# A hybrid decoder step: page loads shared differently between two queues, and four edits of order around them

## The chip, the core and the metric

The kernel runs on one core of a Trainium2 chip. A core has five engines, each with its own instruction queue that is worked in order: TensorE (PE, matmuls), VectorE (DVE), ScalarE (ACT), GpSimd (POOL) and SyncE (SP, which here only issues DMAs). ScalarE and POOL issue DMAs too, between their own instructions. The metric is the device time of one execution in microseconds (us).

## The reference, cut to what matters

One layer of a decoder runs for a prompt of 1024 rows and 8 x 4 sample rows, 1056 in all. Its first half, where the change lies:

```
h = rmsnorm(x, g_norm1) * (1 + scale1) + shift1
za, zq, zkv, zg, zm = jnp.split(h @ w_in, SPLIT_IDX, axis=-1)
u, v = jnp.split(jax.nn.gelu(za), 2, axis=-1)
vn = layernorm(v, ln_v_g, ln_v_b)
ya = chunk_spatial_gating(u, vn, w_spatial, b_spatial)
...
kv_rows = jnp.concatenate([past_rows, paged_new], axis=1)
...
kc = compress_blocks(rows[:, :, :, 0], cmp_pe[0], cmp_w1[0], cmp_b1[0], cmp_w2[0], cmp_b2[0])
vc = compress_blocks(rows[:, :, :, 1], cmp_pe[1], cmp_w1[1], cmp_b1[1], cmp_w2[1], cmp_b2[1])
p_cmp = masked_softmax(jnp.einsum('btkgd,bnkd->btkgn', qg, kc), avail[None, :, None, None, :])
...
gate_a, gate_b = jnp.split(jax.nn.sigmoid(zm), 2, axis=-1)
mixed = (gate_a * (ya @ w_branch_a) + gate_b * (yb @ w_branch_b)) @ w_out
```

For the samples `past_rows` are 8 sequences of 8192 cached rows, and `compress_blocks` makes one key and one value of each 64 rows. The best blocks by `p_cmp` are then attended in full, and a window of 512 rows beside them. After it come the residual, a second norm, the up-projection with a width-3 convolution, the down-projection and a last norm. All is in float32; a big product is made of three float32r products (upper x upper, upper x lower, lower x upper).

## The kernel before, in words

**Compression of the cache (`step`, lines 546 to 664).** The 8 x 8192 cached rows are compressed in 16 steps, numbered 0 to 15. A step takes 32 pages of 128 KB (`pcmp`), all into the one buffer `st`, so the pages of step n+1 are issued only when the 64 matmuls of step n (`compress`) have read it. `step(n)` runs these matmuls, the gelu on ScalarE (`compress_act`, L569), and the issue of the next pages (`compress_load`, `load_pages`, L538). The pages come in eight groups of four. The tuple `share` names the groups that ScalarE issues, (1, 4, 6), and SyncE issues the others. Before, step 5's pages were all left to SyncE. For each group the queue reads four page numbers into registers (L528) and issues four DMAs; a group waits until the group two before it on the same queue has landed, and each issue for an earlier DMA of its lane.

**What lies between the steps.** From about 183 us the u outputs of the gMLP follow (loop with L704 to L722): for each j of 4, 72 products of 384 or 288 columns, then 9 small matmuls of the spatial gating. Steps 3 and 4 stood behind j = 1 and j = 3. Then come 11 pairs (loop at L967) for queries, merge gates and keys. A `pair` makes two outputs of 128 x 1056 by a Strassen-like scheme: the weights' quarters a11, a12, a21, a22 (raw tiles, loaded on ScalarE's queue, L873) give the sums s1 to s4 on POOL (L892 to L897). The activations' quarters give T2, T3, T4 and B12, once (`sums_of`, `last_sums`, on DVE, POOL and ScalarE). Each weight tile is split by a cast on ScalarE (L332) and a subtraction on DVE (L333) into three rotating buffers. A "product" is 12 matmuls: of 304 columns on a quarter, or of 448 on the rest columns (`rest`, `plain`). The scheduler, not the code alone, sets the place of the instructions on each engine. `step(5)` to `step(14)` stand inside pairs 0 to 9, after the a11 and a12 products.

**The start of attention (L1018 to L1063, and from L1209).** The queries lie in memory (`q_d`). The first of the eight tiles of 128 queries is read on its own (`qf`), the four full query tiles `qt` follow, then the values `VV`. `key_tiles` splits the keys, `queries` a tile's queries. The four buffers of `page_buffer` take in turn a chunk of `w_ada` (late modulation), the window cache (`wk`, `wv`) and selected pages (`psel`). Here the code's order holds on TensorE: compressed scores of the first tile, scores of unit 0, unit 1, the first `w_ada` product, and on.

Of the kernel before, what the change touches and what calls it, by code (L numbers as in the profile page):

```python
# [6 lines left out]
F32 = mybir.dt.float32  # L7
# [46 lines left out]
def step_kernel(tc, A):  # L54
# [48 lines left out]
    S = new_pool("slots")  # L103
    NS = 24

    def slot(dt=F32):
        return S([128, R], dt, "S", NS)
# [438 lines left out]
    def compress_load(n):  # L546
        b, half = n // 2, n % 2
        home = "a"
        st = PG([128, 32, 256], F32, "st", 1)
        load_pages([(st[:, i], A["pcmp"], b * 64 + half * 32 + i) for i in range(32)], freed.get(home),  # L550
                   () if n == 5 else (1, 4, 6))
        paged[n] = st, home

    def compress(n):
# [146 lines left out]
    for j in range(4):  # L701
        u = slot()
        dense(A["w_t"][j], 8, hh, hl,
              lambda a, b, ps, u=u: act.activation(u[:, a:b], ps, AF.Gelu_apprx_tanh))  # L704
        for s in range(3):
            w = 512 if s < 2 else 32
            ps = pT()
            tmp = RV2([128, 512], F32, "sg", 2)
            if s < 2:
                for i in range(4):  # L710
                    mm(ps[:, 128 * i:128 * i + 128], vn[4 * s + i][:, 128 * j:128 * j + 128], wsp[:, j], True, True)
                dve.tensor_tensor(tmp.rearrange("p (i t) -> p i t", t=128),
                                  ps.rearrange("p (i t) -> p i t", t=128),
                                  bsp[:, j, None, :].to_broadcast([128, 4, 128]), op=OP.add)
            else:
                mm(ps[:, 0:32], vn[8][:, 128 * j:128 * j + 128], wsps[:, j].rearrange("p b t -> p (b t)"), True, True)
                dve.tensor_tensor(tmp[:, 0:32].rearrange("p (b t) -> p b t", t=4),
                                  ps[:, 0:32].rearrange("p (b t) -> p b t", t=4),
                                  bsp[:, j, None, 0:4].to_broadcast([128, 8, 4]), op=OP.add)
            uc = u[:, 512 * s:512 * s + w]  # L720
            pool.tensor_tensor(uc, uc, tmp[:, 0:w], op=OP.mult)  # L721
        pool.dma_start(ya_d[j], u)  # L722
        if j % 2:
            step(3 + j // 2)
    RV2.release()
    RV.release()
# [131 lines left out]
    def quarter_products(w, x, ps, first, last):  # L858

        for k in range(4):  # L860
            hi, lo = x[k]
            mm(ps, w[0][k], hi, first and k == 0, False, not (first and last))
            mm(ps, w[0][k], lo, False, False, not (first and last))
            mm(ps, w[1][k], hi, False, last and k == 3, not (first and last))

    rest = [tuple(t[:, 2 * HQ:R] for t in (hh[k], hl[k])) for k in range(8)]

    def pair(m, n, ev, closing=False):

        raws = []  # L870
        for j, c in ((m, 0), (m, 512), (n, 0), (n, 512)):
            raws.append(W([128, 512], F32, "raw", 4))
            act.dma_start(raws[-1], A["w_t"][j][:, c:c + 512])  # L873
        a11, a12, a21, a22 = raws
        g, t = out_tile(), out_tile()
        first, second, third = slice(0, HQ), slice(HQ, 2 * HQ), slice(2 * HQ, R)
        plain = [pA()[:, 0:R - 2 * HQ] for _ in range(2)]
        X, S, Z = pA()[:, 0:HQ], pT()[:, 0:HQ], pT()[:, 0:HQ]
        add = lambda o, x, y: dve.tensor_tensor(o, x, y, op=OP.add)  # L879
        s1, s2 = sum_tile(0), sum_tile(1)  # L880

        w = weight_parts(a11)
        quarter_products(w, rest[0:4], plain[0], True, False)
        quarter_products(w, B11, X, True, True)
        act.copy(g[:, first], X)
        w = weight_parts(a12)
        quarter_products(w, rest[4:8], plain[0], False, True)
        quarter_products(w, B21, X, False, True)
        ev(t[:, third], plain[0])
        ev(t[:, first], X)  # L890
        yield
        pool.tensor_tensor(s1, a21, a22, op=OP.add)  # L892
        pool.tensor_tensor(s2, s1, a11, op=OP.subtract)
        quarter_products(weight_parts(a21), rest[0:4], plain[1], True, False)
        s3, s4 = a21, a12
        pool.tensor_tensor(s3, a11, a21, op=OP.subtract)
        pool.tensor_tensor(s4, a12, s2, op=OP.subtract)  # L897
        if closing:
            w = weight_parts(a22)
            quarter_products(w, rest[4:8], plain[1], False, True)  # L900
            ev(g[:, third], plain[1])
            Y = pA()[:, 0:HQ]
            quarter_products(w, T4, Y, True, True)
            quarter_products(weight_parts(s1), B12, Z, True, True)
            ev(g[:, second], Z)
            quarter_products(weight_parts(s4), B22, Z, False, True)
            ev(t[:, second], Z)
            w = weight_parts(s2), weight_parts(s3)
            quarter_products(w[0], T2, S, True, True)
            for o in (t, g):  # L910
                add(o[:, second], g[:, first], o[:, second])
            add(t[:, second], S, t[:, second])
            quarter_products(w[1], T3, S, False, True)
            add(g[:, first], Y, g[:, first])
            add(g[:, second], S, g[:, second])
            add(g[:, first], S, g[:, first])
            yield t, g
            return
        quarter_products(weight_parts(s2), T2, S, True, True)
        add(t[:, second], S, g[:, first])  # L920
        quarter_products(weight_parts(s3), T3, S, False, True)
        add(g[:, second], S, g[:, first])
        quarter_products(weight_parts(s1), B12, Z, True, True)
        add(g[:, second], Z, g[:, second])
        w = weight_parts(a22)
        quarter_products(w, T4, S, False, True)
        add(g[:, first], S, g[:, first])
        ev(g[:, 0:2 * HQ], g[:, 0:2 * HQ])
        quarter_products(w, rest[4:8], plain[1], False, True)
        ev(g[:, third], plain[1])  # L930
        quarter_products(weight_parts(s4), B22, Z, False, True)
        add(t[:, second], Z, t[:, second])
        ev(t[:, second], t[:, second])
        yield t, g
# [32 lines left out]
    for i in range(11):  # L967
        j = 2 * i
        m, fn, ev, base = ((4 + j, query, scaled, 4) if i < 2 else (6 + j, merge_gate, gate, 10) if i < 10 else
                           (8, key, lambda o, x: act.copy(o, x), 8))  # L970
        work = pair(m, m + 1, ev) if i < 10 else pair(9, 8, ev, True)
        next(work)
        if i == 0:
            for k in range(4):
                sums_of(k)
            last_sums()
        if i < 10:
            step(n)
            n += 1
        out = next(work)  # L980
        for x, j in zip(out, (m - base, m + 1 - base)) if i < 10 else zip(out[::-1], range(2)):
            fn(j, x)
        if i in (5, 6, 7, 8):
            next(first_blocks, None)
# [17 lines left out]
    def queries(i, l, qf=None):  # L1002

        c0 = 128 * i
        qs = slot(F32R)
        dve.tensor_copy(qs[0:1, 0:1], l[0:1, 0:1].bitcast(F32))
        for j in range(4):
            q = qf[:, 128 * j:128 * j + 128] if qf is not None else qt[j][:, c0:c0 + 128]
            for h in range(2):
                own, other = slice(64 * h, 64 * h + 64), slice(64 - 64 * h, 128 - 64 * h)  # L1010
                c = (4 * h + j) * 128
                act.copy(qs[own, c:c + 128], q[own])
                dve.tensor_tensor(qs[other, c:c + 128], q[own], qs[own, c:c + 128].bitcast(F32), op=OP.subtract)
        return qs


    qf = W([128, 512], F32, "raw", 4)
    sync.dma_start(qf.rearrange("p (j c) -> p j c", j=4),  # L1018
                   q_d[:, :, 128 * TILES[0]:128 * TILES[0] + 128].rearrange("j p c -> p j c"))
    key_tiles(0)  # L1020
    q_first = queries(TILES[0], KL[0][0], qf)
    compress_act(*compress(15))
    PG.release()
    TR.release()
# [19 lines left out]
    def page_buffer():  # L1044

        n = len(uses)
        uses.append(None)
        assert n < 4 or uses[n - 4] is not None
        return n, R3S([128, 4, 4, 256], F32, f"st{n % 4}", 1), uses[n - 4] if n >= 4 else None

    YS = R3([128, 8, 32])

# [164 lines left out]
    def qtile(i):  # L1217
# [3 lines left out]
        c0 = 128 * i  # L1221
        ps = pM()
        for j in range(4):
            mm(ps[:, 32 * j:32 * j + 32], qt[j][:, c0:c0 + 128], kcb.rearrange("p h n -> p (h n)"), True, True)
        s = R3([128, 8, 16], F32, "cs", 2)
        dve.tensor_tensor(s, ps[:, 0:128].rearrange("p (a n) -> p a n", n=16),
                          cmpadd[:, i, None, :].to_broadcast([128, 8, 16]), op=OP.add)
# [848 lines left out]
```

## Time and profile before

| | us |
|---|---|
| median of three runs | 2006.5 |
| lowest, highest | 2002.08, 2008.75 |
| the profiled execution | 2004.65 |
| its span, first to last instruction | 2003.1 |
| TensorE busy | 1857.2 (93%) |
| DVE, ScalarE, POOL busy | 1240.0, 836.4, 612.4 |
| mean granted TensorE clock | 0.969 of full speed |

A row of the views reads: engine, line of the kernel, operation, output and input tiles, shape, count; in brackets the idle time of the engine before it and what ended it. "ACTq" and "SPq" are the sequencers of ScalarE and SyncE, where DMAs are issued. q1 is SyncE's DMA queue, q10 ScalarE's, q0 POOL's. A window's row gives the stretch, busy time (and count) by engine, the granted clock, the share of the DMA engines and GB/s.

### The profile page before, as it was taken

The page shows a single profiled execution, that of the slowest core. Times are in us where ns is not written, and L with a number is a line of the kernel's source. Part 1 is how long each engine was busy: PE and PEld are TensorE (multiplying, and loading weights), DVE is VectorE, ACT ScalarE, POOL GpSimd, SP SyncE. Part 2 cuts the span into 40 slices and gives each one's busy share as a digit, 9 for nine tenths or more (in the row PEclk, how much of TensorE's full clock was granted, in tenths as well). Part 3 has the DMA queues.
Part 4 walks back from the last instruction along what each step waited for, and adds up shares of the span by engine and source line. Part 5 has one row for each costly group of instructions (what it writes and reads, how often), then busy time and mean ns, then how long its engine had stood idle before and what let it go on. Part 6 is the DMA issues. An engine that isn't in the chain of part 4 may idle for free.

```text
span 2003.1 us, 43803 instructions
## 1 busy us (share of the span) xinstructions
PE 1857.2 (93%) x15905; PEld 1725.1 (86%) x15905; DVE 1240.0 (62%) x2547; ACT 836.4 (42%) x1706; POOL 612.4 (31%) x805
## 2 busy tenths in 40 slices
PE   5999969889989699999999999999999999999998
PEld 3999958878878577676779999999999999999997
DVE  7526163223323476767666667999988888757464
ACT  4313122212222365465564247644444444545343
POOL 2410242112113113223220331188766665301010
PEclk8999989989989799999999999999999999999999
DMA  8546455465564657887775535333322222677464
GB/s 322 186 135 190 139 164 191 144 197 168 164 191 154 225 192 239 285 257 224 228 254 182 200 126 162 113 100 115 108 98 76 86 76 90 212 242 215 138 193 112
DMA packets 241848, 345.36 MB, mean 172 GB/s; under 512 B 35264, under 2 KB 173408, under 8 KB 239456
## 3 DMA queue, kind: packets, MB, share of 16 engines
q1 hardware_dynamic: 186928, 243.17, 38.3%
q0 software_dynamic: 17808, 58.16, 8.1%
q10 hardware_dynamic: 36896, 41.22, 6.6%
q8 instruction: 126, 2.06, 0.5%
q14 instruction: 90, 0.74, 0.1%
HBM read 305.17 MB, written 41.43 MB: 173 GB/s over the span
## 4 chain that ended last, share of the span: by engine, by line
PE 64%; DVE 8%; DMA 6%; ACT 3%; issue 3%; SPq 1%; ACTq 1%; POOL 0%; DVEq 0%
PE t L63 61%; DMA t<-pcmp 4%; PE t L67 3%; DVE t L333 2%; DMA t<-w_ada 1%; ACT t L332 1%; DVE t L1709 1%; DMA t<-t 1%; DVE t L1708 1%; DVE t L1831 1%; DVE t L1756 1%; ACTq L538 1%; ACT t L1288 0%; ACT t L1317 0%; SPq L538 0%
## 5 line engine op out<-in xcount | busy, mean ns | idle before, releaser
L63 PE MATMUL t<-t,t 128*128 128x264 f32 (+13 forms) x15130 | 1782.3, 307 | 131.0 <-ACT t L332 57.8
L63 PEld LDWEIGHTS t<-t,t 128*128 128x128 f32 (+2 forms) x14970 | 1643.6, 170 | 211.1 <-issue 76.1
L332 ACT CAST t<-t 128x512 fp32r<-128x512 f32 (+5 forms) x588 | 335.8, 592 | 582.3 <-PE t L63 335.7
L333 DVE TENSOR_TENSOR t<-t,t 128x512 fp32r<-128x512 f32 (+3 forms) x522 | 429.2, 833 | 232.9 <-ACT t L332 227.2
L879 DVE TENSOR_TENSOR t<-t,t 128x304 f32<-128x304 f32 x55 | 25.9, 473 | 146.4 <-PE t L63 142.1
L1756 DVE TENSOR_TENSOR t<-t,t 128x264 f32<-128x264 f32 (+2 forms) x296 | 92.4, 345 | 28.9 <-PE t L63 27.1
L67 PE MATMUL t<-t,t 128*128 128x128 f32 x746 | 106.5, 278 | 2.8 <-ACT t L1355 1.5
L67 PEld LDWEIGHTS t<-t,t 128*128 128x128 f32 x746 | 80.9, 143 | 32.2 <-issue 8.2
L892 POOL TENSOR_TENSOR t<-t,t 128x512 f32<-128x512 f32 x11 | 14.3, 1303 | 285.6 <-DMA t<-w_t 254.7
L538 POOL DMA_DIRECT2D t<-psel x128 | 70.8, 553 | 69.3 <-DMA t<-psel 28.1
L1910 POOL TENSOR_TENSOR t<-t,t 128x384 f32<-128x384 f32 (+1 forms) x12 | 14.0, 1196 | 223.0 <-ACT t L1977 223.0
L1317 ACT COPY t<-t 128x512 f32<-128x512 f32 (+1 forms) x112 | 59.5, 569 | 36.2 <-PE t L67 36.0
L1709 DVE SCALAR_TENSOR_TENSOR t<-t,t,t 128x1072 f32<-128x1072 f32 x44 | 74.4, 1692 | 0.0
L1287 DVE TENSOR_REDUCE t<-t 128x1 f32<-128x640 f32 (+3 forms) x64 | 58.6, 920 | 22.5 <-PE t L63 22.1
L1707 ACT ACTIVATE t<-t,t 128x1072 f32<-128x1072 f32 x44 | 56.6, 1287 | 37.8 <-DVE t L1756 27.7
L1708 DVE SCALAR_TENSOR_TENSOR t<-t,t,t 128x1072 f32<-128x1072 f32 x44 | 70.4, 1600 | 1.8 <-ACT t L1707 1.7
L1288 ACT ACTIVATE t<-t,t 128x640 f32<-128x640 f32 (+3 forms) x64 | 56.2, 879 | 23.9 <-DVE t L1287 21.3
L1813 POOL TENSOR_TENSOR t<-t,t 128x1024 f32<-128x1024 f32 x22 | 55.1, 2506 | 20.2 <-ACT t L1812 20.2
L1344 POOL COPY t<-t 128x256 f32<-128x256 f32 x32 | 12.9, 402 | 147.1 <-DVE t L1342 62.4
L1703 POOL COPY t<-t 128x2 f32<-128x2 f32 x44 | 34.7, 788 | 52.3 <-DVE t L1756 52.3
L721 POOL TENSOR_TENSOR t<-t,t 128x512 f32<-128x512 f32 (+1 forms) x12 | 11.7, 992 | 125.8 <-ACT t L332 86.9
L1587 POOL TENSOR_TENSOR t<-t,t 128x384 f32<-128x384 f32 (+1 forms) x24 | 27.9, 1167 | 64.6 <-DVE t L1586 61.4
(293 smaller groups left out, 1377.9 us busy)
## 6 DMA issues: line engine op xcount, KB each, us to landing
t<-psel SPq DMA_DIRECT2D x384, 128.0 KB
t<-pcmp SPq DMA_DIRECT2D x332, 128.0 KB
t<-w_down SPq DMA_DIRECT2D x120, 256.0 KB
t<-t POOLq DMA_DIRECT2D x54, 528.0 KB, 3.3
t<-w_up SPq DMA_DIRECT2D x96, 256.0 KB
t<-pcmp ACTq DMA_DIRECT2D x180, 128.0 KB
t<-psel POOLq DMA_DIRECT2D x128, 128.0 KB, 4.0
t<-w_ada SPq DMA_DIRECT2D x16, 1024.0 KB
```

Of the source, the lines that this page charges most:

```text
L63: return pe.matmul(out, lhsT, rhs, start=start, stop=stop, skip_group_check=skip)
L67: return pe.transpose(out, x, ident)
L332: act.copy(hi, t)
L333: dve.tensor_tensor(lo, t, hi.bitcast(F32), op=OP.subtract)
L538: d = queue.dma_start(dst, src[bass.ds(r, 1)].rearrange("g p c -> p (g c)"))
L1287: dve.tensor_reduce(m4[:, branch, h:h + 1], ps[:, :, 0:w], axis=AX.XY, op=OP.max, negate=True)
L1288: act.activation(P[:, 0:L].rearrange("p (a c) -> p a c", a=2), ps[:, :, 0:w], AF.Exp, bias=m4[:, branch, h:h + 1], accum_out=s4[:, branch, ...
L1317: (act.copy if w > 2 else dve.tensor_copy)(probs[branch, h][:, 128 * k:128 * (k + w)], pt[:, c:c + 128 * w])
L1707: act.activation(acc[:, 0:w], up[:, 0:w], AF.Identity, scale=cw[:, n, 0:1], bias=cw[:, n, 3:4])
L1708: dve.scalar_tensor_tensor(acc[:, 0:w], up[:, 1:1 + w], cw[:, n, 1:2], acc[:, 0:w], op0=OP.mult, op1=OP.add)
L1709: dve.scalar_tensor_tensor(acc[:, 0:w], up[:, 2:2 + w], cw[:, n, 2:3], acc[:, 0:w], op0=OP.mult, op1=OP.add)
L1756: dve.tensor_tensor(o, by4(banks[c][:, c0:c0 + n], n), other(c, c0, n), op=OP.add)
```

## The change

There are five edits. ScalarE issues groups 1 and 4 of every step, SyncE the other six. Steps 3 and 4 stand behind u outputs 0 and 2. In the first pair (`opening`) both rest products of a21 and a22 come ahead of the step and of T2; a22 is split twice there. In the pairs 1 to 9 the T2 product comes ahead of the rest products of a21; the last pair (`closing`) keeps its order. The first query tile goes to a slot, not to a weight buffer, is split before the keys, and serves the first compressed scores; in return each of the four first page buffers gets a one-element copy on POOL that reads the last query tile, so that loads over that element come after it.

```diff
@@ compress_load
         load_pages([(st[:, i], A["pcmp"], b * 64 + half * 32 + i) for i in range(32)], freed.get(home),
-                   () if n == 5 else (1, 4, 6))
+                   (1, 4))
@@ u outputs
         pool.dma_start(ya_d[j], u)
-        if j % 2:
+        if j % 2 == 0:
             step(3 + j // 2)
@@ pair
-    def pair(m, n, ev, closing=False):
+    def pair(m, n, ev, opening=False, closing=False):
...
         pool.tensor_tensor(s1, a21, a22, op=OP.add)
         pool.tensor_tensor(s2, s1, a11, op=OP.subtract)
-        quarter_products(weight_parts(a21), rest[0:4], plain[1], True, False)
+        if opening or closing:
+            quarter_products(weight_parts(a21), rest[0:4], plain[1], True, False)
+        if opening:
+            quarter_products(weight_parts(a22), rest[4:8], plain[1], False, True)
+            ev(g[:, third], plain[1])
+            yield
+        if not (opening or closing):
+            quarter_products(weight_parts(s2), T2, S, True, True)
+            add(t[:, second], S, g[:, first])
+            quarter_products(weight_parts(a21), rest[0:4], plain[1], True, False)
         s3, s4 = a21, a12
...
-        quarter_products(weight_parts(s2), T2, S, True, True)
-        add(t[:, second], S, g[:, first])
+        if opening:
+            quarter_products(weight_parts(s2), T2, S, True, True)
+            add(t[:, second], S, g[:, first])
         quarter_products(weight_parts(s3), T3, S, False, True)
...
-        quarter_products(w, rest[4:8], plain[1], False, True)
-        ev(g[:, third], plain[1])
+        if not opening:
+            quarter_products(w, rest[4:8], plain[1], False, True)
+            ev(g[:, third], plain[1])
@@ loop over pairs
-        work = pair(m, m + 1, ev) if i < 10 else pair(9, 8, ev, True)
+        work = pair(m, m + 1, ev, i == 0) if i < 10 else pair(9, 8, ev, False, True)
         next(work)
         if i == 0:
             for k in range(4):
                 sums_of(k)
+            next(work)
             last_sums()
@@ queries
-        dve.tensor_copy(qs[0:1, 0:1], l[0:1, 0:1].bitcast(F32))
+        if qf is None:
+            dve.tensor_copy(qs[0:1, 0:1], l[0:1, 0:1].bitcast(F32))
@@ first query tile
-    qf = W([128, 512], F32, "raw", 4)
+    qf = slot()[:, 0:512]
     sync.dma_start(qf.rearrange("p (j c) -> p j c", j=4),
                    q_d[:, :, 128 * TILES[0]:128 * TILES[0] + 128].rearrange("j p c -> p j c"))
+    q_first = queries(TILES[0], None, qf)
     key_tiles(0)
-    q_first = queries(TILES[0], KL[0][0], qf)
@@ page_buffer
-        return n, R3S([128, 4, 4, 256], F32, f"st{n % 4}", 1), uses[n - 4] if n >= 4 else None
+        st = R3S([128, 4, 4, 256], F32, f"st{n % 4}", 1)
+        if n < 4:
+            pool.tensor_copy(st[0:1, 0, 0, 0:1], qt[3][0:1, 0:1])
+        return n, st, uses[n - 4] if n >= 4 else None
@@ qtile
-            mm(ps[:, 32 * j:32 * j + 32], qt[j][:, c0:c0 + 128], kcb.rearrange("p h n -> p (h n)"), True, True)
+            q = qf[:, 128 * j:128 * j + 128] if i == TILES[0] else qt[j][:, c0:c0 + 128]
+            mm(ps[:, 32 * j:32 * j + 32], q, kcb.rearrange("p h n -> p (h n)"), True, True)
```

How this moves instructions is seen in three places. The first is ScalarE in pair 1, from the gelu of a step (L569) to the casts of s1, a22 and s4 (L332) and the next weight loads (L873). Each L528 opens a group of four page DMAs (L538). Before:

```order
L569 ACTIVATE t_4107<-t_4035,t_594 128x64x2
L528 TENSOR_LOAD t_543
...
L528 TENSOR_LOAD t_543
...
L528 TENSOR_LOAD t_543
...
L332 CAST t_4268<-t_3974 128x512
L332 CAST t_4285<-t_3965 128x512
L332 CAST t_4316<-t_3961 128x512
L873 DMA t_4344<-w_t 128x512
L873 DMA t_4346<-w_t 128x512
```

And of the change, at the same place:

```order
L569 ACTIVATE t_4111<-t_4039,t_594 128x64x2
L528 TENSOR_LOAD t_543
...
L528 TENSOR_LOAD t_543
...
L332 CAST t_4272<-t_3978 128x512
L332 CAST t_4289<-t_3969 128x512
L332 CAST t_4320<-t_3965 128x512
L873 DMA t_4348<-w_t 128x512
L873 DMA t_4350<-w_t 128x512
```

The third group is gone from between the gelu and the casts; the rest stands as it did.

The second place is TensorE in the first pair. t_3508 is the bank of the rest products of a21 and a22, t_3509 that of B21, t_3510 that of T2; t_3654 and t_3689 are the banks of compression 5, and its rows of 16 end it. Before:

```order
L63 MATMUL t_3508<-t_576,t_3836 128x448
L63 MATMUL t_3510<-t_3473,t_3853 128x304
L63 MATMUL t_3510<-t_3474,t_3853 128x304
L63 MATMUL t_3654<-t_3351,t_546 64x128 x2
...
L63 MATMUL t_3654<-t_3351,t_549 64x128 x16
L63 MATMUL t_3510<-t_3473,t_3854 128x304
```

And of the change:

```order
L63 MATMUL t_3509<-t_580,t_3544 128x304
L63 MATMUL t_3508<-t_577,t_3651 128x448
...
L63 MATMUL t_3508<-t_580,t_3652 128x448
L63 MATMUL t_3689<-t_3238,t_546 64x128 x2
...
L63 MATMUL t_3689<-t_3238,t_549 64x128 x16
L63 MATMUL t_3510<-t_3473,t_3870 128x304
```

The first two T2 matmuls stood ahead of the compression; now the a22 products (t_3651, t_3652) and the whole compression stand ahead of T2.

The third place is SyncE at the start of attention: the small query tile, then w_ada, the window cache (wk, wv), the four query tiles (128x1056) and the values (o_rows). Before:

```order
L1018 DMA t_7659<-t_3465 128x4x128
L1205 DMA t_7909<-w_ada 128x2048 x2
L1061 DMA t_8097<-wk 128x4x512
L1063 DMA t_8097<-wv 128x4x128 x2
L1031 DMA t_7786<-t_3465 128x1056
...
L1031 DMA t_7789<-t_3465 128x1056
L1034 DMA t_7794<-o_rows 128x4x256
L1034 DMA t_7795<-o_rows 128x4x256
L1063 DMA t_8097<-wv 128x4x128 x2
```

And of the change (lines are 13 to 16 higher in it):

```order
L1031 DMA t_7663<-t_3465 128x4x128
L1221 DMA t_7912<-w_ada 128x2048
L1079 DMA t_8101<-wv 128x4x128
L1044 DMA t_7789<-t_3465 128x1056
...
L1044 DMA t_7792<-t_3465 128x1056
L1047 DMA t_7797<-o_rows 128x4x256
L1047 DMA t_7798<-o_rows 128x4x256
L1079 DMA t_8101<-wv 128x4x128 x3
L1221 DMA t_7912<-w_ada 128x2048
L1077 DMA t_8101<-wk 128x4x512
```

One half of w_ada, wk and most of wv have moved behind the query tiles and the values; the other half of w_ada still stands ahead of them.

## The prediction

> **What bounds the kernel now.** I read the page first. TensorE is busy 93% of the span, and its clock line dips in the slices between 250 and 700 us, so I asked which waits TensorE has from 140 to 700 us.
>
> ```profile
> PEclk8999989989989799999999999999999999999999
> PE t L63 <- ACT t L332: 55.6, 11, 12.4
> PE t L63 <- DMA t<-t: 18.9, 4, 16.9
> PE t L63 <- DVE t L879: 3.7, 6, 0.7
> ```
>
> Eleven waits of 55.6 us in all end with a cast of ScalarE (L332, the upper part of a weight tile). One of them is 12.4 us long, in the first pair; the other ten share 43.2 us, one for each later pair step. The 18.9 us on a DMA are the start of attention. Everything that the change touches lies here. The timeline of a middle pair shows what the cast waits for, on ScalarE and TensorE:
>
> ```profile
> 434.70 0.50 ACT L569 ACTIVATE t<-t,t 128x128 f32<-128x128 f32 x1 [6.11 <-PE t L63]
> 435.36 10.01 ACTq L538 DMA_DIRECT2D t<-pcmp  x12
> 439.64 1.92 PE L63 MATMUL t<-t,t 128*128 128x304 f32 x12 [0.66 <-DVE t L879]
> 445.41 1.14 ACT L332 CAST t<-t 128x512 fp32r<-128x512 f32 x2 [10.21 <-DMA t<-pcmp]
> 446.08 0.62 PE L63 MATMUL t<-t,t 128*128 128x304 f32 x1 [4.51 <-ACT t L332]
> 441.92 3.44 ACTq L538 DMA_DIRECT2D t<-pcmp  x4
> ```
>
> When the compression is done (L569), ScalarE issues twelve page loads in 10.01 us, and four of them, the third group, from 441.92 on; an issue itself takes about 0.35 us, the rest is waiting for earlier page loads. The cast of the next weight tile stands behind them. TensorE has three products of 12 matmuls whose weights were cast before; it ends them at 439.64 + 1.92 = 441.56 and then waits 4.51 us.
>
> A wait costs more than itself:
>
> ```profile
> 300.00:304.00 4.00, 3.89 (x14) 0.50 0.91 269
> 304.00:308.00 4.00, 4.00 (x26) 1.00 0.68 234
> 277.64:284.64 7.00, 7.00 (x73) 0.58 0.22 77
> 300.11:307.11 7.00, 7.00 (x32) 0.72 0.89 281
> 446.08:453.08 7.00, 7.00 (x32) 0.67 0.82 266
> 629.64:636.64 7.00, 7.00 (x30) 0.61 0.84 268
> 439.64:441.56 1.92, 1.92 (x12) 1.68 (x12) 0.00 (x0) 0.00 (x0) 0.00 (x0) 1.00 0.94 298
> ```
>
> In these windows the column after the matmuls (in the last row after all five engines) is the granted clock. After the wait that ends at 300.11 TensorE runs at half clock, 14 matmuls in 4 us where the next 4 us have 26. Over the 7 us after each of the eleven waits the clock falls short of 1 by 0.42 (the first, 277.64), 0.28, ... to 0.39 (the last, 629.64), together 3.44, so 3.44 x 7 = 24.1 us are lost, 2.9 of them after the first. After the 0.66 us wait at 439.64 the clock stayed at 1.00.
>
> **The change part by part**, against the profiled execution (2004.65 us, span 2003.1; the median of the three runs, 2006.5, is 1.85 higher).
>
> *ScalarE's third group.* From 441.4 (its register load, just ahead of the 441.92 row) to 445.41 it holds ScalarE 4.0 us. The order shows it gone and the same three products in front of the wait, so each of the ten waits shrinks by about 4.0: **-40 us**. What is late next is the cast behind the second group, at 441.4 + 0.6, still 0.5 us after TensorE has run dry. If nothing were left it would be -43; if the second group then waits longer, half of it, -20. Since 0.66 us left the clock alone, the half clock after these ten goes too: 24.1 - 2.9 = **-21 us** (0 if waits of over 3 us stay).
>
> *SyncE's sixth group.* The pages of a step are still 32 x 128 KB = 4.2 MB, and SyncE now issues 24 in place of 20. They must be complete when the next compression begins.
>
> ```profile
> q1 hardware_dynamic: 4587, 4.18, 73.0%
> q1 hardware_dynamic: 1597, 1.45, 49.9%
> q10 hardware_dynamic: 1469, 1.34, 41.4%
> 434.70:463.40 28.70, 23.53 (x138) 21.77 (x138) 8.78 (x15) 7.11 (x13) 6.95 (x6) 0.88 0.66 209
> t<-t POOLq DMA_DIRECT2D x54, 528.0 KB, 3.3
> ```
>
> The first row is SyncE's queue from 255 to 275 us, where it loads a whole step alone: 4.18 MB in 20 us, 209 GB/s. The next two are both queues from 436 to 446: 145 and 134 GB/s. So ScalarE's 8 pages (1.05 MB) take 7.8 us; SyncE has moved 1.16 MB by then and needs 9.5 us for the other 1.99 MB, 17.5 in all. Two weight loads on ScalarE's queue (0.52 MB, 3.9 us at 134) hold SyncE to 145 meanwhile: +1.2. The two 528 KB stores of a pair add up to 2.9 us if they fall inside (1.08 MB at the 370 GB/s of the attention start below). That is 18.7 to 21.6 us, plus about 1 to start and to land. The window from one compression to the next is 28.70 now (the 434.70 row); without 4.0 of waiting and without 7 x 0.33 = 2.3 of half clock it is 22.4. So the pages come in just about time. I take 0.5 us a step, **+5 us** for ten; the bounds are 0 and 4 us a step with the half clock back, from SyncE held to 145 throughout (3.15 / 0.145 = 21.7, + 2.9 + 1 = 25.6).
>
> [...]
>
> *The opening pair.*
>
> ```profile
> 244.66 1.79 ACTq L873 DMA_DIRECT2D t<-w_t  x4
> 247.52 1.31 ACT L332 CAST t<-t 128x512 fp32r<-128x512 f32 x2 [2.51 <-DMA t<-w_t]
> 250.87 0.46 DVE L832 TENSOR_TENSOR t<-t,t 128x304 f32<-128x304 f32 x1
> 276.97 0.62 ACT L332 CAST t<-t 128x512 fp32r<-128x512 f32 x1 [0.68 <-POOL t L893]
> 277.64 0.62 PE L63 MATMUL t<-t,t 128*128 128x304 f32 x1 [12.37 <-ACT t L332]
> ```
>
> The first T2 product needs s2, which POOL makes behind the sums of the activations; the chain runs from 250.87 to 276.97, 26.1 us, and TensorE waits 12.37 for it. Two things are put into the wait: the a22 products (12 matmuls, 2 us at 0.16 us each, as 26 in 4 us above) and compression 5 (64 half-width matmuls, about 8 us). But compression 4 moves from just ahead of the pair into the u outputs (below), and there it covered the load of the first weights (244.66 to 247.52) and the start of the chain. Counted from the end of the last u product: before, T2 starts at 277.64 - 244.6 = 33.0 with compression 4 done; after, 8 later for compression 4, then the chain starts at about 4.3, takes 26.1, and the cast stands behind eight page issues, about 2: 8 + 32.5 = 40.5, with 10 us more work done. Gain 10 - 7.5 = **-2.5 us**; bounds 0 and -15 (12.37 + 2.9, all covered). a22 is split a second time, one cast and one subtraction (0.6 and 0.7 us) inside the chain.
>
> *Steps behind other u outputs.*
>
> ```profile
> 68.22 192.10 PE L63 MATMUL t<-t,t 128*128 128x262 f32 x1906 [1.32 <-ACT t L491]
> ```
>
> TensorE does not wait from 68 to 260 us, so nothing can be won. A step now has one u output and part of the next ahead of it, about 72 + 44 matmuls and 9 small ones, some 20 us, where a load takes 18.7 to 21.6: **0 us**, at worst +3 twice.
>
> *Product order in a middle pair.* T2 now comes ahead of the a21 products. Its s2 is ready 28 us before, as POOL's sums follow the loads of a21 and a22 at once; the work is the same: **0**, bounds -3.7 and +3.7 (the 0.66 us waits doubled or gone).
>
> *First query tile.*
>
> ```profile
> 667.27 1.05 ACT L995 CAST t<-t 64x1024 fp32r<-64x1024 f32 x1 [5.12 <-DVE t L879]
> 669.99 0.83 SPq L1205 DMA_DIRECT2D t<-w_ada  x2
> 670.86 0.43 SPq L1061 DMA_DIRECT2D t<-wk  x1
> 671.34 2.54 SPq L1063 DMA_DIRECT2D t<-wv  x2
> 673.92 7.26 SPq L1031 DMA_DIRECT2D t<-t  x4
> 686.81 0.61 PE L63 MATMUL t<-t,t 128*128 128x32 f32 x2 [16.86 <-DMA t<-t]
> 678.86 0.69 DVE L998 CAST t<-t 64x1024 fp32r<-64x1024 f32 x1
> 699.12 2.23 PE L63 MATMUL t<-t,t 128*128 128x320 f32 x18
> 671.00:689.00 18.00, 1.24 (x4) 1.00 (x4) 7.48 (x15) 7.35 (x14) 3.23 (x6) 0.55 1.03 370
> ```
>
> TensorE stands from 669.95 to 686.81 until the queries (L1031) have come in behind w_ada, wk and wv. Read from the small tile, it can start at once, and scores follow as key tiles are made (667.27 to 679.55). The next thing late is w_ada: its first product is in the 699.12 row, and half of w_ada now comes behind the queries, because the new POOL copy holds it. Ahead of and with that half SyncE moves 6.36 MB (by the tile shapes: 1.05 w_ada, 0.26 wv, 2.16 queries, 1.05 values, 0.79 wv, 1.05 w_ada), and POOL 1 MB of psel: 7.4 MB at 370 GB/s is 20 us from 670, so 691 where 699.4 was. **-8 us**; bounds 0 and -19 (all of the 18.9). POOL's four copies wait for the queries with the later norm copies and psel issues behind them; these are due after w_ada.
>
> Sum: -40 - 21 + 5 - 2.5 + 0 + 0 - 8 = -66.5; 2004.65 - 66.5 = 1938, and by the median 1940.
>
> **The rivals.** *The pages become the bound:* a wait of 2 to 4 us a step on a page load in place of ScalarE's. For it speaks that the load (up to 25.6) and the window (22.4) are near. It gives 20 to 40 us in place of 5, and at the upper end the clock falls again:
>
> ```profile
> 482.25 1.15 PE L63 MATMUL t<-t,t 128*128 128x304 f32 x3 [3.32 <-ACT t L332]
> 482.25:489.25 7.00, 7.00 (x29) 0.57 0.92 289
> ```
>
> After 3.32 us the clock was at 0.57 for 7 us. 1955 to 1995. *Everything is covered:* no page wait, the opening wait gone, the query start at its bound: -43 - 21 - 15 - 19 gives 1907, by the median 1908. *The change doesn't do what it says:* the wait moves to the second group, which waits for the first as the third did, 20 of the 40 us stay and most of the half clock: about 1970. The order shows the casts behind eight issues, against it. *Slower:* SyncE's queue cannot carry 24 pages beside the other traffic. It decides where a load passes 27.7 us, the 28.70 window less 1: 3.15 MB at 114 GB/s. At 100 it is 31.5 us, 3.8 longer than now in each of ten steps, no wait gained, +38 and 2045 in the end. Its lowest row is 145, so this is unlikely.
>
> **How the numbers follow.** Forecast (gains 45 to 90 us, centre 1940) 0.74; pages the bound 0.14; all covered 0.07; second group 0.03; slower 0.02. Own range of the forecast 1916 to 1961; with most of the page rival and the edge of the covered one 1912 to 1980. About 0.3% (6 us) is what a measurement can tell from no change. Faster 0.95, same 0.02 (the top of the page rival with the rest lost), slower 0.03.
>
> **What would show it.** In the profile after: ten waits on L332 of 0.5 us and the clock line near full from 300 to 670 us; a pair step of about 31 us (36.6 now: 300.11 to 629.64 over nine); a small wait on pcmp ahead of compressions; a wait on w_ada near the start of attention in place of that on the queries; a wait of some 6 us for s2 in the first pair. Waits on pcmp of over 2 us a step, or half clock between them, would make the number wrong.

## The result, and the profile after

The changed kernel takes **1953.03 us** (median of 4 runs, 1951.54 to 1956.6) where the kernel before took 2005.34 beside it: a ratio of 0.9742, 95% interval 0.9719 to 0.9764. That is 52 us less. The forecast was 66.5 less (1940); the range of 1912 to 1980 holds the result. The profiled run has a span of 1952.5 us, where before had 2003.1. In the table of the experiments one run of e14, 2553.65 us at a granted clock of 0.654, is left out of its median.

The clock line of its page:

```profile
PEclk9999989999999899999999999999999999999999
```

TensorE's waits from 250 to 660 us in the changed kernel (total, how often, longest):

```profile
PE t L63 <- ACT t L332: 28.7, 11, 14.4
PE t L63 <- DMA t<-w_ada: 7.5, 1, 7.5
PE t L63 <- ACT t L1305: 4.6, 1, 4.6
```

The waits on ScalarE's cast have gone from 55.6 to 28.7 us, and half of what is left is one wait, that of the first pair. No wait on a page load (pcmp) and none on VectorE's L879 is among them. The dips of the clock between 300 and 620 us are gone from the line.

From the end of the first pair's second wait to the end of the pairs' products, the kernel before (length, busy times of TensorE, its weight loads, VectorE, ScalarE and GpSimd, clock, DMA share, GB/s):

```profile
300.11:669.95 369.84, 329.52 (x2773) 307.12 (x2773) 115.03 (x202) 87.65 (x161) 75.19 (x72) 0.93 0.52 167
```

and the same stretch of the changed kernel:

```profile
301.62:625.97 324.35, 313.05 (x2774) 290.93 (x2774) 123.28 (x208) 89.32 (x167) 75.12 (x74) 0.99 0.58 188
```

The same matmuls take 45.5 us less: 369.84 - 329.52 = 40.3 us of idle time became 324.35 - 313.05 = 11.3, so 29.0 are waits, and 16.5 are busy time that a clock of 0.99 in place of 0.93 makes shorter.

What remains in the pairs, on TensorE's timeline of the changed kernel:

```profile
301.62 25.75 PE L63 MATMUL t<-t,t 128*128 128x448 f32 x244 [0.57 <-ACT t L332]
329.42 30.09 PE L63 MATMUL t<-t,t 128*128 128x304 f32 x268 [2.05 <-ACT t L332]
361.28 31.66 PE L63 MATMUL t<-t,t 128*128 128x304 f32 x268 [1.78 <-ACT t L332]
394.61 30.28 PE L63 MATMUL t<-t,t 128*128 128x304 f32 x268 [1.68 <-ACT t L332]
585.75 14.58 PE L63 MATMUL t<-t,t 128*128 128x304 f32 x84 [1.53 <-ACT t L332]
```

From 329.42 to 585.75 there are eight steps of 32.0 us, where a step was 36.6. Each still has a wait of 0.4 to 2 us. One of them, on ScalarE and TensorE:

```profile
386.98 0.49 ACT L569 ACTIVATE t<-t,t 128x128 f32<-128x128 f32 x1 [5.89 <-PE t L63]
387.71 6.19 ACTq L538 DMA_DIRECT2D t<-pcmp  x8
393.94 1.66 ACT L332 CAST t<-t 128x512 fp32r<-128x512 f32 x3 [6.47 <-DMA t<-pcmp]
394.61 2.19 PE L63 MATMUL t<-t,t 128*128 128x304 f32 x11 [1.68 <-ACT t L332]
```

Eight page loads hold ScalarE from 387.71 to 393.9, though an issue takes 0.34 us (the median of the 72 on ScalarE's queue from 300 to 600 us); the cast comes behind them.

With marks that are in both traces (the activation of a compression, L569; the waits above; the first copy of the w_ada stage, L263) the whole change splits up like this; the forecast's terms stand beside it:

| stretch (before, after) | before us | after us | change | forecast |
|---|---|---|---|---|
| to the activation of step 2 (183.3, 182.8) | 183.3 | 182.8 | -0.5 | 0 |
| to the end of the first pair's second wait (300.11, 301.62) | 116.8 | 118.8 | **+2.0** | -2.5 - 4.0 = -6.5 |
| to the end of the pairs (669.95, 625.97) | 369.8 | 324.4 | -45.5 | -36 - 21 + 5 = -52 |
| to the first w_ada copy (701.5, 651.9) | 31.6 | 25.9 | -5.6 | -8 |
| to the end of the span | 1301.6 | 1300.6 | -1.0 | 0 |

### The profile page after: what moved, and what is told of

It reads as the page before. It is cut to its first block, busy times and chain, and to the rows that moved or that the text cites. A ratio compares the mean times of both kernels' runs of the same rounds, so it can differ in the third digit from the quotient of the medians.

```text
span 1952.5 us, 43825 instructions
## 1 busy us (share of the span) xinstructions
PE 1843.3 (94%) x15905; PEld 1707.8 (87%) x15905; DVE 1247.9 (64%) x2547; ACT 837.7 (43%) x1707; POOL 612.7 (31%) x809
## 4 chain that ended last, share of the span: by engine, by line
PE 74%; DVE 8%; DMA 6%; issue 4%; ACT 4%; POOL 2%; SPq 1%; ACTq 0%; DVEq 0%; POOLq 0%
PE t L63 70%; PE t L67 3%; DMA t<-pcmp 2%; DVE t L333 2%; DMA t<-t 1%; ACT t L332 1%; DVE t L1725 1%; DMA t<-psel 1%; DMA t<-o_rows 1%; DMA t<-w_up 1%; DVE t L1726 0%; ACT t L1305 0%; DVE t L823 0%; ACT t L1334 0%; POOL t L1751 0%
## 5 line engine op out<-in xcount | busy, mean ns | idle before, releaser
L63 PE MATMUL t<-t,t 128*128 128x264 f32 (+12 forms) x15130 | 1768.0, 306 | 94.3 <-ACT t L332 30.9
L63 PEld LDWEIGHTS t<-t,t 128*128 128x128 f32 (+2 forms) x14970 | 1625.7, 169 | 176.9 <-issue 59.7
L332 ACT CAST t<-t 128x512 fp32r<-128x512 f32 (+5 forms) x589 | 336.9, 592 | 522.9 <-PE t L63 312.3
L333 DVE TENSOR_TENSOR t<-t,t 128x512 fp32r<-128x512 f32 (+5 forms) x523 | 432.6, 838 | 181.4 <-ACT t L332 174.2
L1773 DVE TENSOR_TENSOR t<-t,t 128x264 f32<-128x264 f32 (+2 forms) x296 | 92.3, 345 | 27.9 <-PE t L63 25.7
L879 DVE TENSOR_TENSOR t<-t,t 128x304 f32<-128x304 f32 x55 | 25.8, 472 | 115.7 <-PE t L63 112.2
L538 POOL DMA_DIRECT2D t<-psel x128 | 70.7, 553 | 77.4 <-DMA t<-psel 38.2
L1304 DVE TENSOR_REDUCE t<-t 128x1 f32<-128x640 f32 (+3 forms) x64 | 58.7, 920 | 34.1 <-PE t L63 33.8
L1830 POOL TENSOR_TENSOR t<-t,t 128x1024 f32<-128x1024 f32 x22 | 54.6, 2480 | 20.5 <-ACT t L1829 20.5
L1604 POOL TENSOR_TENSOR t<-t,t 128x384 f32<-128x384 f32 (+1 forms) x24 | 27.9, 1166 | 66.4 <-DVE t L1603 63.3
```

The source lines that it names most:

```text
L63: return pe.matmul(out, lhsT, rhs, start=start, stop=stop, skip_group_check=skip)
L332: act.copy(hi, t)
L333: dve.tensor_tensor(lo, t, hi.bitcast(F32), op=OP.subtract)
L538: d = queue.dma_start(dst, src[bass.ds(r, 1)].rearrange("g p c -> p (g c)"))
L1304: dve.tensor_reduce(m4[:, branch, h:h + 1], ps[:, :, 0:w], axis=AX.XY, op=OP.max, negate=True)
L1773: dve.tensor_tensor(o, by4(banks[c][:, c0:c0 + n], n), other(c, c0, n), op=OP.add)
```

## The experiments

Ratios are to the kernel before, run on the same chip beside each; its medians there were 2003.1 to 2005.7 us.

| run | what it is | median us | ratio | 95% interval |
|---|---|---|---|---|
| change | | 1953.03 | 0.9742 | 0.9719 to 0.9764 |
| e1 | before, shares (1, 4) only | 1949.97 | 0.9734 | 0.9712 to 0.9756 |
| e2 | change, shares as before | 2002.82 | 0.9994 | 0.9982 to 1.0006 |
| e3 | before, query tile only | 2001.11 | 1.0002 | 0.9987 to 1.0017 |
| e11 | before, shares and query tile | 1948.78 | 0.9716 | 0.9694 to 0.9739 |
| e7 | change, old product order | 1949.15 | 0.9731 | 0.9701 to 0.9762 |
| e8 | change, step 6's pages on SyncE | 1948.20 | 0.9720 | 0.9702 to 0.9738 |
| e9 | e8, s2 cast first | 1951.48 | 0.9730 | 0.9690 to 0.9771 |
| e5 | change, one group from step 7 | 1925.23 | 0.9612 | 0.9582 to 0.9643 |
| e6 | change, no group from step 7 | 1926.61 | 0.9612 | 0.9577 to 0.9648 |
| e12 | e5 and e8 | 1921.38 | 0.9586 | 0.9560 to 0.9612 |
| e14 | before, query tile, shares of e12 | 1937.68 | 0.9646 | 0.9613 to 0.9680 |
| e16 | e12, old product order | 1942.24 | 0.9688 | 0.9652 to 0.9724 |

### Which edit carries the gain (e1, e2, e3, e11)

e1 is the kernel before with this alone:

```diff
-                   () if n == 5 else (1, 4, 6))
+                   () if n == 5 else (1, 4))
```

> The kernel before with one edit alone: ScalarE issues the page groups 1 and 4, not 6 (the step whose pages SyncE loads alone is left as it is). Theory (the third group set the ten pair waits, and the rest of the change is worth about 10 us): about 1963 us, 1956 to 1970; ten pair waits on L332 of 1 to 2 us in place of 4.3 and a pair step of about 32 us. Rival (the new product order and places of the steps were needed for it): waits of 3 us or more remain, pair step 34 us or more, 1980 or more.

e2 is the changed kernel with the reverse of the diff's first line:

```diff
-                   (1, 4))
+                   () if n == 5 else (1, 4, 6))
```

> The changed kernel with the old shares (groups 1, 4 and 6, and none in the step ahead of the first pair), all other edits kept. Theory: the ten waits of 4 us and their half clock are back, and only the query tile (about 8) and the rest (about 2) are left of the gain: 1993 to 1999 us, pair step 36.5. Rival (order edits carry part of the gain in the pairs): 1975 to 1985, pair step under 35.5.

One tuple is the whole gain: e1 gives 0.0266 x 2003.1 = 53.3 us, e2 keeps 1.2 of them (interval -1.2 to 3.6). Both theories had been too kind to the rest: e1 was to leave 10 us to the other edits and left none. In e2 the waits on L332 between 300 and 660 us are 42.3 us, before they were 43.2.

e3 is the kernel before with the edits of the first query tile (its load into `slot()`, `queries` ahead of `key_tiles(0)`, the GpSimd copies in `page_buffer`, the first compressed scores from that tile, the copy in `queries` left out):

> The kernel before with the first query tile read on its own and nothing else. Theory: the 16.9 us wait on the queries goes, a wait of about 7.5 us on w_ada comes in its place, gain 7 to 9 us: 1996 to 1999 us. Rival (the start of attention is held by w_ada and the queries behind it all the same): within 2 us of the kernel before, 2003 to 2007.

In e3 TensorE's waits from 660 to 720 us begin with these; the four on the queries, 18.9 us, are gone:

```profile
PE t L63 <- DMA t<-w_ada: 7.2, 1, 7.2
PE t L63 <- ACT t L1293: 4.6, 1, 4.6
```

So at its place the mechanism is as expected, with a smaller size: from the last store of keys (o_k) to the first w_ada copy it is 33.7 us before and in e1, and 28.7 in e3, e2 and e11, 5.0 less each time (29.4 in the changed kernel). In the run's time e3 does not show it: the interval reaches from 2.6 us faster to 3.4 slower and holds neither 5 nor the 7 to 9 expected. The traces show where it goes: from the activation of step 2 to that store e3 takes 489.4 us, where before takes 484.5, so at the w_ada copy both are level (518.1 and 518.2). These 4.9 us can be half clock, of which e3 has 78.5 us in this stretch and before 68.3, in one profile of each. But e11 too takes 3.3 us longer than e1 there (437.4 and 434.1), with the same 20.5 us of half clock in both. Whether the edit itself lengthens the pairs stays open.

e11 has the shares of e1 and the query tile of e3:

> The kernel before with two edits: ScalarE's groups 1 and 4, and the first query tile read on its own; the steps, the first pair and the product order as before. Theory (by the marks of the profiles: the new opening and the moved steps cost about 4 us against the old ones, the query tile is worth 4.6 us at the first w_ada product): 1943 to 1947 us, less than the changed kernel. Rival (opening and moves are worth nothing either way): 1950 to 1953. Second rival (the query tile gives nothing in the end): 1949 to 1951, as with the shares alone.

It lies between theory and second rival: by the ratios 3.6 us under e1, where the query tile was added, and 5.2 under the changed kernel, which has the new opening and the moved steps besides. Both intervals overlap, so the whole-run times alone don't settle it. The profiles point the same way: in e1 the first pair's second wait is over at 293.35, in e11 at 296.45,

```profile
293.35 27.88 PE L63 MATMUL t<-t,t 128*128 128x304 f32 x244 [3.32 <-ACT t L332]
```

(e1's row). Counted from the activation of step 2 that is 112.3 us in e1 (181.04 to 293.35) and 113.6 in e11 (182.81 to 296.45), where it is 116.8 before and 118.8 in the changed kernel. So the shares alone win 4.5 us here, and with the other edits 2.0 are lost: the new opening and the moved steps cost some 5 to 6.5 us, in one profile each. (The pages of step 5 differ too: SyncE alone loads them in e1 and e11.) At the first w_ada copy 3.0 of this are left: it comes 466.1 us after the activation in e11 and 469.1 in the changed kernel. In e1 it comes after 467.7. So by these marks the query tile and the new opening nearly cancel, and the change with and without them comes out alike.

### The product order (e7)

```diff
-        if opening or closing:
-            quarter_products(weight_parts(a21), rest[0:4], plain[1], True, False)
+        quarter_products(weight_parts(a21), rest[0:4], plain[1], True, False)
...
-        if not (opening or closing):
-            quarter_products(weight_parts(s2), T2, S, True, True)
-            add(t[:, second], S, g[:, first])
-            quarter_products(weight_parts(a21), rest[0:4], plain[1], True, False)
...
-        if opening:
-            quarter_products(weight_parts(s2), T2, S, True, True)
-            add(t[:, second], S, g[:, first])
+        quarter_products(weight_parts(s2), T2, S, True, True)
+        add(t[:, second], S, g[:, first])
```

> The changed kernel with the old order of products in the middle pairs (a21 ahead of T2). Theory (forecast of 0): within 3 us of 1953; the waits of 0.66 us on VectorE (L879) come back, six of them, 3.7 us, and nothing else. Rival (the new order shortens the wait behind the second group): 1960 or more, waits on L332 over 2.5 us.

TensorE's waits of e7 from 250 to 660 us:

```profile
PE t L63 <- ACT t L332: 26.6, 12, 14.6
PE t L63 <- DVE t L879: 3.7, 6, 0.7
```

The six waits on L879 are back, 3.7 us, and those on the cast are 2.1 us less: where VectorE does not hold TensorE, TensorE runs dry sooner and waits more than half of it out at ScalarE. The time is 0.9731 where the change has 0.9742: no change.

### The first pair (e8, e9)

```diff
-                   (1, 4))
+                   () if n == 6 else (1, 4))
```

> The changed kernel, but the pages that the step in the first pair loads are all issued by SyncE, so that no page issue stands ahead of the cast of s2 on ScalarE. Theory (the cast, ready at 285.3 and done at 293.5, was held by page issues): TensorE's wait in the first pair falls from 14.4 to 6 to 9 us, and the time by 6 to 8: about 1946 us. Rival A (the casts of the last sums, which wait for VectorE and GpSimd, hold it as well): wait of 11 us or more, time within 3 us of 1953. Rival B (SyncE's pages come late for compression 6): a wait on pcmp in the second pair, time 1953 or more.

GpSimd (which makes s2) and ScalarE in the first pair of the changed kernel:

```profile
283.83 1.43 POOL L893 TENSOR_TENSOR t<-t,t 128x512 f32<-128x512 f32 x1 [0.80 <-DVE t L823]
284.52 0.48 ACT L569 ACTIVATE t<-t,t 128x128 f32<-128x128 f32 x1
284.98 0.85 ACTq L538 DMA_DIRECT2D t<-pcmp  x2
288.10 0.45 ACT L822 CAST t<-t 128x304 fp32r<-128x304 f32 x1 [3.10 <-DVE t L850]
288.23 0.84 ACTq L538 DMA_DIRECT2D t<-pcmp  x2
...
292.00 0.85 ACTq L538 DMA_DIRECT2D t<-pcmp  x2
292.89 0.62 ACT L332 CAST t<-t 128x512 fp32r<-128x512 f32 x1 [0.59 <-issue]
```

and in e8:

```profile
283.06 0.48 ACT L569 ACTIVATE t<-t,t 128x128 f32<-128x128 f32 x1
283.83 0.62 ACT L332 CAST t<-t 128x512 fp32r<-128x512 f32 x1 [0.29 <-POOL t L893]
```

In the changed kernel s2 is made at 285.26 and its cast starts at 292.89, 7.6 us later. The cast stands behind eight page issues, and between these the scheduler has put casts of the last sums (L822), which wait for VectorE. Behind the first two issues ScalarE waits 3.1 us for such a sum. In e8 the cast starts at 283.83, as soon as GpSimd has made s2 (ScalarE idles 0.29 us for it), and TensorE's waits are:

```profile
PE t L63 <- ACT t L332: 21.0, 12, 7.1
PE t L63 <- DMA t<-w_t: 3.3, 1, 3.3
```

The longest wait falls from 14.4 to 7.1 us as the theory has it, and not to rival A's 11 or more. But in e8 the scheduler has also put the casts of the remaining sums behind that of s2, so the run takes both away and doesn't part the issues from these casts. Of the 7 us 3.3 come back one compression later than rival B said: TensorE waits that long until 342.82, ahead of compression 7. The time is 0.972, 4 us less, with overlapping intervals.

e9 also makes the parts of s2 ahead of the `yield` at which the step stands:

```diff
             ev(g[:, third], plain[1])
+            w2s = weight_parts(s2)
             yield
...
-            quarter_products(weight_parts(s2), T2, S, True, True)
+            quarter_products(w2s, T2, S, True, True)
```

> The changed kernel with the first pair's s2 cast and split ahead of the step in the order of the code, and with the step's pages all issued by SyncE. Theory (queue order on ScalarE is all that holds the cast): cast at about 285.5, wait of TensorE about 6 to 7 us in place of 14.4, time about 1945. Rival (the next product, with s3, then waits in its place): first wait 6, a second one of 4 or more, time within 3 us of 1953.

It adds nothing to e8 (longest wait 7.9 us, and 3.2 on w_t); the cast could not come sooner, since s2 was made at 287.05 and the cast starts at 287.09.

### What is left in the pairs (e5, e6)

```diff
-                   (1, 4))
+                   (1, 4) if n < 7 else (1,))
```

> The changed kernel, but from step 7's pages on ScalarE issues one group of four and SyncE 28 pages. Theory (what is left of the pair waits, 1 to 2 us each, is ScalarE held by its second group; SyncE still has time): waits on L332 under 0.5 us, no wait on pcmp, pair step 30.5 to 31 us, time 1936 to 1945. Rival (the pages are now the bound): waits of TensorE on pcmp of 1 us or more a step, time 1953 or more.

```diff
-                   (1, 4))
+                   (1, 4) if n < 7 else ())
```

> The changed kernel, but from step 7's pages on SyncE issues all 32. At 209 GB/s a load takes 20 us, with the weight loads and stores beside it 22 to 25; a pair step without waits gives it about 22. Theory (SyncE's queue is near its limit): waits on pcmp of 1 to 3 us a step, time 1945 to 1965, not better than with one group. Rival (its queue has time to spare): no wait on pcmp, no wait on L332, 1932 to 1942.

Both give 0.9612, 26 us less than the change, more than any expectation had. ScalarE in a step of e5:

```profile
385.33 0.49 ACT L569 ACTIVATE t<-t,t 128x128 f32<-128x128 f32 x1 [7.78 <-PE t L63]
385.99 1.87 ACTq L538 DMA_DIRECT2D t<-pcmp  x4
387.90 0.62 ACT L332 CAST t<-t 128x512 fp32r<-128x512 f32 x1 [2.07 <-DMA t<-pcmp]
```

and TensorE's waits in e5 from 300 to 590 us, where the changed kernel has 11.4 us on L332:

```profile
PE t L63 <- DMA t<-pcmp: 1.3, 2, 0.7
PE t L63 <- ACT t L332: 0.8, 2, 0.6
```

Four issues hold ScalarE 1.9 us where eight hold it 6.2: the second group is what waits for the first. So the 11.4 us were the second group. From the start of the first pair to the first w_ada product e5 is 25.2 us shorter; idle time is 13.3 of that, and busy time for the same 3076 matmuls 11.9, of which at most 4.1 is half clock (34.6 us of it in this stretch, where the changed kernel has 42.8). The other 8 us I cannot assign. In e6 TensorE has two waits on pcmp, 7.7 us in all, and the time is no better than e5's: SyncE alone is just about enough.

### Two gains together, and what they rest on (e12, e14, e16)

```diff
-                   (1, 4))
+                   (1, 4) if n < 6 else () if n == 6 else (1,))
```

> The changed kernel with SyncE alone loading the pages of step 6 and one group of ScalarE's from step 7 on. Theory (the two gains, 4 us in the first pair and 26 us in the others, add up): 1919 to 1923 us. Rival (they overlap, since the first pair's gain is taken up in a later wait): 1925 to 1928.

1921.38 us: 0.9586, the fastest of all, and as the theory has it. Its interval and that of e5 overlap (0.9582 to 0.9612), so that the first pair's 4 us come on top is likely and not shown.

e14 puts the same shares, and SyncE alone in step 5, into the kernel before with the query tile:

```diff
-                   () if n == 5 else (1, 4, 6))
+                   (1, 4) if n < 5 else () if n in (5, 6) else (1,))
```

> The kernel before with the query tile and new shares alone: SyncE loads the pages of steps 5 and 6, ScalarE one group from step 7 on; steps, first pair and product order as before. Theory (the old opening is no worse than the new one, and only the shares matter): 1917 to 1922 us, within 3 us of the changed kernel with the same shares. Rival (the new opening or product order pays once ScalarE is free): 1927 or more.

It came out at 0.9646, some 12 us over e12 (0.0060 x 2003): the rival. Which edit it was, e16 tells, which is e12 with the diff of e7:

> The changed kernel with the pages of step 6 on SyncE and one group of ScalarE's from step 7 on, and the product order of the middle pairs put back (a21 ahead of T2). Theory (with the new order the compressions stand later in each step, by up to 29 products, and the pages have more time; with the old order they must be there after one pair): waits on pcmp and w_t of 1 to 2.5 us in half the steps, 1930 to 1940 us. Rival (the product order is worth nothing here too, and the opening or the moved steps made the difference between the two kernels with these shares): 1919 to 1925.

The theory: 0.9688, 20 us slower than e12 by the product order alone. That is more than the 12 us of e14, which has the old order too: e14 is 8 us under e16, with overlapping intervals, and differs from it in opening, places of the steps and step 5's pages. TensorE's waits of e16 from 300 to 590 us:

```profile
PE t L63 <- DMA t<-w_t: 11.3, 5, 3.8
PE t L63 <- DMA t<-pcmp: 3.0, 2, 1.5
```

and of e12 from 300 to 580 us:

```profile
PE t L63 <- DMA t<-pcmp: 1.3, 1, 1.3
PE t L63 <- DMA t<-w_t: 0.3, 1, 0.3
```

In e16 a wait stands ahead of the compression in nearly every step, as these rows of its timeline show (the 128*64 128x128 form begins a compression):

```profile
372.94 29.31 PE L63 MATMUL t<-t,t 128*64 128x128 f32 x268 [1.41 <-DMA t<-pcmp]
404.52 30.95 PE L63 MATMUL t<-t,t 128*64 128x128 f32 x268 [2.27 <-DMA t<-w_t]
439.22 32.55 PE L63 MATMUL t<-t,t 128*64 128x128 f32 x278 [3.75 <-DMA t<-w_t]
```

A compression multiplies pages with weights loaded long before, so the waits put down to w_t are waits on pages too. The trace bears that out: at all five, the last page load of the step lands 0.24 to 0.30 us ahead of the first matmul (at 404.28 for the row of 404.52), as it does at the wait on pcmp that ends at 342.23 (341.99); the weight load beside it lands with only 0.01 to 0.13 us left. Of the 20 us, some 13 are these waits, and at most 5 half clock (10.2 us of it in e16 from 305 to 590, none in e12). In the order of TensorE's instructions e16 has 132 matmuls of the pairs from one compression to the next (e14 nearly always too), e12 mostly 142 to 149. So with the new product order the scheduler lets each compression slip a little later, by 10 to 17 matmuls of 0.16 us (12 took 1.92 in the kernel before), and pages that SyncE brings almost alone have more time, by an estimate from these counts about 2 us. It does so only with the new shares: in the changed kernel itself most steps have 132 as well. That this slip is what saves the 20 us is argued from these orders, not shown by a run of its own. The edit that e7 found worth nothing is worth 20 us with these shares, where the pages are the bound.

## Why the prediction was right, and where its sizes were off

**The third group** was the right cause: e1 alone gives 53.3 us, and the prediction's three terms for it, -40 - 21 + 5, come to 56. That they agree so well is partly luck, since each was off:

- *Ten waits shrink by 4.0 us.* The idle time of the stretch of nine waits fell by 29.0, not 36. ScalarE is free 6.96 us after the activation begins (386.98 to 393.94), close to the 6.7 reckoned (434.70 to 441.4), but TensorE runs dry sooner, 5.95 us after it (392.93) in place of 6.86 (441.56): the 0.66 us waits on L879 were counted as part of its work, and most of them moved to the cast (e7).
- *Half clock, -21.* Busy time fell by 16.5. Behind two waits, of 1.78 us (to 361.28) and 1.62 (to 426.52), the granted clock still went to half, for 3.41 us each time.
- *SyncE's sixth group, +5.* It cost nothing: no wait on pcmp. (In the working, 7.8 and 9.5 us add up to 17.3, not 17.5; nothing hangs on it.) The "pages are the bound" rival was wrong for this kernel, and becomes right with one group and the old product order (e16).

**The opening pair** is the step that failed: -2.5 in the sum, and a loss of 5 to 6.5 measured (+2.0 in the table's second stretch, where the shares alone win 4.5 and shares and query tile 3.2). The prediction put the cast of s2 behind "eight page issues, about 2" and the wait at some 6 us; the cast came 7.6 us after s2 and the wait was 14.4. It had priced an issue and not what stands between the issues in ScalarE's order, casts that wait for other engines. The chain up to s2 took 27.9 us (257.34 to 285.26) in place of 26.1. So T2 starts 39.8 us behind the last u product (253.78 to 293.56), not 32.5. e8 shows 7.1 with the issues, and the casts between them, out of the way.

**First query tile, -8.** The mechanism is right (w_ada in place of the queries), and the size at its place was 4.3 to 5.6, by the mark that one counts from. SyncE in the changed kernel shows what the sum left out:

```profile
624.26 0.35 SPq L1221 DMA_DIRECT2D t<-w_ada  x1
624.66 0.42 SPq L1079 DMA_DIRECT2D t<-wv  x1
...
628.42 2.63 SPq L1047 DMA_DIRECT2D t<-o_rows  x2
631.86 8.38 SPq L1079 DMA_DIRECT2D t<-wv  x3
641.27 0.42 SPq L1221 DMA_DIRECT2D t<-w_ada  x1
```

The sum had the bytes run at 370 GB/s up to w_ada's second half. That half is issued only at 641.27, behind three wv loads that hold SyncE for 8.4 us, and its first product runs at 648.21, 22.2 us after the end of the pairs. The run of e3 cannot be told from no change, that of e11 is 3.6 us under e1 with overlapping intervals, and in both traces the pairs ahead of it are longer by 3 to 5 us.

**Product order: 0.** Right for this change (e7), and only for it (e16). **Steps behind other u outputs: 0.** TensorE has no wait there in the changed kernel either; the moved steps were not run without the new opening, so what each has of the 5 to 6.5 us is open. e2, with all edits but the shares, is at 0.9994.

## What to carry to other kernels

Price a group of DMA issues on a busy engine by how long the group holds it, up to the next thing that others wait for, with all that the scheduler has put between the issues; here the third group cost about 53 us, and the second, with a product order that leaves room for the pages, another 26. Try an edit again after the bound has moved: the product order was worth nothing under one bound and 20 us under the next. And where several edits come together, run each alone: here one carried all, and by the marks of the traces two others nearly cancelled.

## What the runs showed of the hardware that was not expected

In the changed kernel the granted clock went to half behind waits much shorter than I had reckoned with, of 1.78 us (to 361.28) and 1.62 (to 426.52), and stayed at 1.00 behind others as long, of 2.05 (to 329.42) and 1.68 (to 394.61): it depended on when they came. In the profiles of before and of the change it changes only at the edges of a grid of 3.41 us, in the change for instance at 363.06, 366.48, 427.92 and 431.33; each stretch of one clock, but for the last of the span, is a whole number of 3.41 us long. Four cells of that grid (to within 0.1 us), and the one behind each, in the changed kernel (TensorE's busy time is the first after the length; the clock is the third number from the end):

```profile
325.46:328.87 3.41, 1.91 (x14) 1.64 (x12) 0.47 (x1) 0.12 (x1) 0.00 (x0) 1.00 0.87 278
328.87:332.28 3.41, 2.86 (x18) 2.60 (x19) 1.90 (x3) 1.63 (x4) 0.00 (x0) 1.00 0.78 233
359.61:363.02 3.41, 1.74 (x9) 1.48 (x10) 2.16 (x4) 1.66 (x3) 0.00 (x0) 1.00 0.99 325
363.02:366.43 3.41, 3.41 (x16) 3.41 (x15) 1.23 (x3) 0.62 (x1) 0.00 (x0) 0.51 0.87 254
390.32:393.73 3.41, 2.62 (x17) 2.30 (x15) 0.47 (x1) 0.00 (x0) 0.00 (x0) 1.00 0.96 313
393.73:397.14 3.41, 2.53 (x15) 2.27 (x16) 1.90 (x3) 1.66 (x3) 0.00 (x0) 1.00 0.88 254
424.45:427.86 3.41, 1.79 (x11) 1.28 (x10) 1.84 (x4) 1.66 (x3) 0.00 (x0) 1.00 0.90 272
427.86:431.27 3.41, 3.41 (x15) 3.41 (x14) 1.27 (x3) 0.62 (x1) 0.00 (x0) 0.51 0.90 281
```

The wait of 1.78 us that ends at 361.28 lies in one cell but for its first 0.1 us; the cell is busy for 1.74 us, and the next cell runs at half clock. The wait of 2.05 that ends at 329.42 and that of 1.68 that ends at 394.61 fall across an edge, and the clock stays at 1.00. In the two profiles, from 300 to 600 us, the ten full-clock cells with 1.8 us of busy time or less (eight before, two in the change) were followed by half clock, and none of those with 1.85 or more was; outside this stretch two cells of the change with 1.45 and 1.64 us (from 277.7 and 663.4) were followed by full clock. The half clock of the same code varied too: the pairs of e3 are those of the kernel before, and between 305 and 590 us its profile has 41.0 us of half clock where that of before has 34.1.
